# Moving the copies of bias rows and past cache behind each block's first-matrix products

## The chip, the cores and the metric

One core of one Trainium2 chip runs the whole program. The metric is device time in microseconds of one execution. The kernel before took 2709.98 us, the median of 3 runs that spread from 2709.81 to 2712.33 us.

## The reference, cut to what matters

The reference is one step of a two-layer decoder trunk on 1088 tokens (1024 of a prompt, 64 of eight running sequences) of width 1024. Layer 0 mixes with gated linear attention, layer 1 with sliding-window attention over 128 keys with a relative-position bias; both then have a squared-ReLU MLP of inner width 4096 and a gated per-layer input embedding. What the change touches is this part:

```
h = h + y                                                   # the mixer's result
h = h + square(relu(rmsnorm(h) @ w_up[i])) @ w_down[i]      # the MLP
gate = sigmoid(rmsnorm(h) @ w_ple_gate[i])
h = h + gate * (p[i] @ w_ple[i])                            # p: the per-layer input
...
bias = rel_bias.T[:, rel_bucket(max(d, 0))]                 # of layer 1's attention logits
new_k = concatenate([past_k, k_sh])[:, -n_past:]            # 120 past rows are kept, v alike
```

## The kernel before, in words

All activations are held transposed, 128 features by 1088 tokens a tile. Every product is made of three float32r products: weights and activations are split into a high and a low half, and `mm3` (L186) issues high by high (L189), high by low (L190) and low by high (L191) into the same sum. A weight tile comes by one DMA from SP into a raw buffer (2 of them), ACT casts the high half (L142), and VectorE subtracts to get the low half (L143); 5 buffers each hold the halves. `wnext` (L169) hands out the next weight tile, and fills the line so that three more tiles behind it have been asked for.

The MLP of a layer (`mlp`, L817) runs over 8 blocks of 512 inner features. A block has two parts. The first-matrix part is two calls of `up_pair` (L741). One call uses, in this order, the weight tiles A1, S2S1, C1, S4S3, A22 and C2, most of them sums of raw tiles that VectorE forms at L161 to L166; ACT and VectorE turn its results into the activations `us` (L770 to L774). The second-matrix part has eight tiles, here called down 0 to down 7, each with 36 products of 362 or 364 columns; VectorE adds each result into the residual `H` at L841, three pieces a tile. The eighth block also squares the new residual for the norm (L248, L251, L252), splits it (L221, L222) and, ahead of its second-matrix part in the program, opens the per-layer input (`ple_open`, L851): two tiles `praw` are loaded into one buffer, one after the other, each split by ACT at L218 and VectorE at L219.

In layer 0 each block also issues `bias_copies` (L929): one DMA from SP that writes two heads' bias rows 128 times (0.39 MB, memory to memory) into `ed`; the eighth block adds two copies of 120 past rows of the caches (0.98 MB each) to the outputs. GpSimd reads `ed` later in `sample_bias`, and layer 1's attention reads it.

What sets the order: `load` (L76 to L83) ties each DMA that it issues to the one before it,

```
r = self.nc.sync.dma_start(out, in_)
if self.last_load is not None:
    self.order(r.ins, self.last_load)
```

so SP issues all of them in the order of the program text. For the compute engines the framework's scheduler fixes the order of each engine's instructions when the program is built: it walks the program in its own picture of time and lets an instruction pass an earlier one that isn't ready in that picture. On the chip every engine runs its list strictly in that order.

Of the kernel before, what the change touches and what calls it, by code (L numbers as in the profile page):

```python
# [47 lines left out]
class Trunk:  # L48
# [768 lines left out]
    def mlp(self, layer, gain, utag, tags):  # L817
        nc = self.nc
        xs, rb = self.hg, self.rb
        self.hg = []  # L820
        self.pq = self.wide("pq")
        self.xz = self.rs.tile([P, TP], F32, tag="acc", name=self.uid("xz"), bufs=1)
        pt = ("mm", "gx")
        for fb in range(FB):
            us = []
            if layer == 0:
                self.bias_copies(fb)
            for f in range(0, FT, 2):
                us += [self.double(utag) for _ in range(2)]
                self.up_pair(layer, fb * FT + f, xs, us[f:])  # L830
            if fb == FB - 1:
                self.norm_begin()
                self.stx.close()
                self.ple_open(layer)
            for j in range(KT):
                ws = self.wtile([("down", layer, fb, j)])
                h = self.h[j]

                def evac(c0, cn, ps):
                    s = slice(c0, c0 + cn)  # L840
                    nc.vector.tensor_tensor(h[:, s], h[:, s], ps, op=ALU.add)  # L841
                self.gemm(ws, us, evac, kouter=(j == 0), tags=pt)
                if fb == FB - 1:
                    self.norm_add(h)
                    d = self.double(tags[j // 4])
                    self.split(d, h, self.gain(gain, j), CH if j >= 6 else ((0, T),))
                    self.hg.append(d)
        self.norm_end()
# [546 lines left out]
```

## Time and profile before

| | |
|---|---|
| median of the runs | 2709.98 us |
| profiled execution | 2710.06 us |
| its span | 2708.3 us |
| TensorE busy | 2665.8 us, 98% |
| VectorE busy | 1735.6 us, 64% |
| ScalarE (ACT) busy | 1162.2 us, 43% |
| GpSimd busy | 127.5 us, 5% |
| DMA | 163.56 MB, mean 60 GB/s |
| mean granted clock of TensorE | 0.997 of full |

The profiled execution lasts 1.8 us longer than its span, which runs from the first to the last instruction; the sum of the prediction starts from 2710.06 us. PE is TensorE's matmul, DVE is VectorE, ACT is ScalarE, POOL is GpSimd, SP the engine that issues most DMAs. A busy share says how full an engine is, not who waits: for that the list of waits, the timeline of each engine and the busy time of equal stretches are read. The layer 0 MLP lies at about 562 to 1319 us, the layer 1 MLP at about 1829 to 2571 us.

### The profile page before, as it was taken

The numbers are of one execution on the slowest core, as the hardware profiler recorded it, in microseconds if no ns is written. First come the engines' busy times: TensorE is split into PE (matmuls) and PEld (weight loads), VectorE is DVE, ScalarE is ACT, GpSimd is POOL, SyncE is SP. The second block draws the span as 40 slices with busy tenths as digits, with TensorE's granted clock in tenths as the row PEclk, the third lists the DMA queues.
The fourth block names the chain that finished last, engine by engine and source line by source line (L and its number), as shares of the span: only waits on it lengthen the run. The fifth ranks groups of instructions, "written<-read, shape, count | busy, mean of one in ns | idle before, by whom it ended". The sixth has DMA issues, their size and how long they took to land.

```text
span 2708.3 us, 46678 instructions
## 1 busy us (share of the span) xinstructions
PE 2665.8 (98%) x18369; PEld 2595.9 (96%) x18369; DVE 1735.6 (64%) x4377; ACT 1162.2 (43%) x2694; POOL 127.5 (5%) x154
## 2 busy tenths in 40 slices
PE   9999999999999999999999999999999999999997
PEld 8999999999999999999999988799999999999997
DVE  5787786584565466456755677676655655565787
ACT  5565576351232233124524666554322322332565
POOL 0000000001001000010000333200000000000000
PEclk9999999999999999999999999999999999999999
DMA  3121112311111121122122111222111111111252
GB/s 126 40 65 42 57 46 72 104 47 47 57 55 35 57 62 36 46 88 63 52 81 64 50 37 49 63 69 59 40 43 48 55 34 50 51 46 34 67 179 98
DMA packets 92801, 163.56 MB, mean 60 GB/s; under 512 B 11558, under 2 KB 30650, under 8 KB 92549
## 3 DMA queue, kind: packets, MB, share of 16 engines
q1 hardware_dynamic: 89637, 155.20, 18.6%
q10 hardware_dynamic: 1152, 4.46, 0.5%
q8 instruction: 144, 2.36, 0.4%
q0 software_dynamic: 1792, 0.92, 0.2%
q14 instruction: 76, 0.62, 0.1%
HBM read 145.95 MB, written 19.98 MB: 61 GB/s over the span
## 4 chain that ended last, share of the span: by engine, by line
PE 94%; DVE 3%; ACT 2%; issue 0%; DMA 0%; POOL 0%; DVEq 0%; SPq 0%; ACTq 0%; POOLq 0%
PE mm L191 20%; PE mm L189 20%; PE mm L190 20%; PE gx L191 8%; PE gx L190 8%; PE gx L189 8%; PE gx L549 2%; PE gx L1162 1%; PE gx L1148 1%; PE gx L578 1%; PE gx L573 1%; PE gs L1131 1%; PE gx L580 0%; PE gs L257 0%; PE gs L1132 0%
## 5 line engine op out<-in xcount | busy, mean ns | idle before, releaser
L189 PE MATMUL mm<-G,whi 128*128 128x362 f32 (+2 forms) x3160 | 1014.2, 322 | 15.7 <-ACT whi L142 9.5
L191 PE MATMUL mm<-G,wlo 128*128 128x362 f32 (+2 forms) x3160 | 1012.6, 320 | 0.8
L190 PE MATMUL mm<-G,whi 128*128 128x362 f32 (+2 forms) x3160 | 1010.8, 320 | 0.0
L189 PEld LDWEIGHTS mm<-G,whi 128*128 128x128 f32 x3160 | 594.8, 188 | 23.6 <-ACT whi L142 11.8
L191 PEld LDWEIGHTS mm<-G,wlo 128*128 128x128 f32 x3160 | 594.4, 188 | 5.4 <-DVE wlo L143 2.8
L190 PEld LDWEIGHTS mm<-G,whi 128*128 128x128 f32 x3160 | 594.9, 188 | 3.5 <-issue 1.7
L191 PE MATMUL gx<-G,wlo 128*128 128x272 f32 (+2 forms) x1304 | 397.5, 305 | 0.0
L190 PE MATMUL gx<-G,whi 128*128 128x272 f32 (+2 forms) x1304 | 397.4, 305 | 0.0
L189 PE MATMUL gx<-G,whi 128*128 128x272 f32 (+2 forms) x1304 | 397.1, 305 | 0.0
L142 ACT CAST whi<-raw 128x512 fp32r<-128x512 f32 (+1 forms) x304 | 187.2, 618 | 398.8 <-PE mm L190 318.2
L841 DVE TENSOR_TENSOR H<-H,mm 128x364 f32<-128x364 f32 (+1 forms) x256 | 135.9, 531 | 227.0 <-PE mm L191 226.3
L143 DVE TENSOR_TENSOR wlo<-raw,whi 128x512 fp32r<-128x512 f32 (+1 forms) x304 | 208.5, 687 | 73.5 <-ACT whi L142 72.7
L190 PEld LDWEIGHTS gx<-G,whi 128*128 128x128 f32 x1304 | 246.1, 189 | 0.1
L191 PEld LDWEIGHTS gx<-G,wlo 128*128 128x128 f32 x1304 | 246.1, 189 | 0.0
L189 PEld LDWEIGHTS gx<-G,whi 128*128 128x128 f32 x1304 | 245.9, 189 | 0.1
L772 ACT ACTIVATE tmp<-tmp 128x272 f32<-128x272 f32 x256 | 109.5, 432 | 270.5 <-DVE tmp L771 269.1
L841 DVE TENSOR_TENSOR H<-H,gx 128x362 f32<-128x362 f32 x128 | 68.0, 531 | 137.3 <-PE gx L191 137.2
L774 DVE TENSOR_TENSOR G<-tmp,G 128x272 fp32r<-128x272 f32 x256 | 111.5, 439 | 59.5 <-ACT G L773 58.7
L142 ACT CAST whi<-sum 128x512 fp32r<-128x512 f32 x64 | 39.5, 618 | 178.0 <-PE mm L190 150.3
L771 DVE SCALAR_TENSOR_TENSOR tmp<-tmp,rb 128x272 f32<-128x272 f32 x256 | 110.9, 437 | 3.7
L251 ACT ACTIVATE tmp<-H 128x362 f32<-128x362 f32 (+1 forms) x126 | 63.6, 507 | 114.0 <-DVE H L678 57.3
L773 ACT CAST G<-tmp 128x272 fp32r<-128x272 f32 x256 | 106.2, 419 | 5.2
(295 smaller groups left out, 4057.1 us busy)
## 6 DMA issues: line engine op xcount, KB each, us to landing
raw<-in_w_down SPq DMA_DIRECT2D x128, 256.0 KB
a<-in_w_up SPq DMA_DIRECT2D x64, 256.0 KB
raw<-in_w_up SPq DMA_DIRECT2D x64, 256.0 KB
G<-in_w_gate SPq DMA_DIRECT2D x24, 512.0 KB
raw<-in_w_o SPq DMA_DIRECT2D x32, 256.0 KB
raw<-in_w_q SPq DMA_DIRECT2D x24, 256.0 KB
x<-in_xT ACTq DMA_DIRECT2D x8, 544.0 KB
hd<-H SPq DMA_DIRECT2D x8, 544.0 KB
```

The costliest lines, as they stand in the source:

```text
L142: nc.scalar.copy(hi[:, s], raw[:, s])
L143: nc.vector.tensor_tensor(lo[:, s], raw[:, s], hi[:, s].bitcast(F32), op=ALU.subtract)
L189: mm(out, lhsT=w[0], rhs=x[0], start=first, stop=False)
L190: mm(out, lhsT=w[0], rhs=x[1], start=False, stop=False)
L191: mm(out, lhsT=w[1], rhs=x[0], start=False, stop=last)
L251: nc.scalar.activation(sq[:, :cn], h[:, s], AF.Square)
L549: nc.tensor.matmul(pp[:m, l * hw:(l + 1) * hw], lhsT=E[:, l, :m], rhs=ev[:, :, 1, :], start=True, stop=True)
L771: nc.vector.scalar_tensor_tensor(t, t, 0.0, rb[:, s], op0=ALU.max, op1=ALU.mult)
L772: nc.scalar.activation(t, t, AF.Square)
L773: nc.scalar.copy(u[:, 0, s], t)
L774: nc.vector.tensor_tensor(u[:, 1, s], t, u[:, 0, s].bitcast(F32), op=ALU.subtract)
L841: nc.vector.tensor_tensor(h[:, s], h[:, s], ps, op=ALU.add)
```

## The change

The call of `bias_copies` moves, within a block of layer 0's MLP, from ahead of the two `up_pair` calls to behind them. Nothing is added or removed.

```
         for fb in range(FB):
             us = []
-            if layer == 0:
-                self.bias_copies(fb)
             for f in range(0, FT, 2):
                 us += [self.double(utag) for _ in range(2)]
                 self.up_pair(layer, fb * FT + f, xs, us[f:])
+            if layer == 0:
+                self.bias_copies(fb)
             if fb == FB - 1:
                 self.norm_begin()
                 self.stx.close()
                 self.ple_open(layer)
```

By the order of the program, SP issues a block's copy before between the load of the first call's C1 and that of its C2, and with the change between the load of down 2 and that of down 3; in the eighth block the loads of `praw` come between the copies and down 3.

## Rows read from the trace of the kernel before

**Rows 1.** Page, the chain that ended last, by engine.

```profile
PE 94%; DVE 3%; ACT 2%; issue 0%; DMA 0%; POOL 0%; DVEq 0%; SPq 0%; ACTq 0%; POOLq 0%
```

**Rows 2.** Waits of PE, 560 to 1290: us in total, times, longest.

```profile
PE mm L189 <- ACT whi L142: 9.5, 8, 1.3
```

**Rows 3.** Stretches, one block each, layer 0 then layer 1: length, then engines' busy time.

```profile
615.00:709.79 94.79, 93.53 (x650) 93.10 (x649) 52.47 (x116) 26.62 (x60) 6.91 (x12) 1.00 0.17 50
...
1877.34:1970.33 92.99, 92.99 (x650) 92.99 (x649) 52.94 (x116) 27.09 (x60) 0.00 (x0) 1.00 0.16 46
```

**Rows 4.** Timeline of PE, layer 0: start, duration, what, idle before and its releaser.

```profile
671.48 0.29 PE L191 MATMUL gx<-tx,wlo 128*128 128x272 f32 x1
672.94 0.40 PE L189 MATMUL mm<-G,whi 128*128 128x272 f32 x1 [1.18 <-ACT whi L142]
...
673.30 0.28 PE L189 MATMUL gx<-G,whi 128*128 128x272 f32 x1
673.67 0.40 PE L191 MATMUL mm<-G,wlo 128*128 128x272 f32 x1
```

**Rows 5.** Timeline of ACT, the same moment.

```profile
671.95 0.42 ACT L773 CAST G<-tmp 128x272 fp32r<-128x272 f32 x1
672.28 0.61 ACT L142 CAST whi<-raw 128x512 fp32r<-128x512 f32 x1
```

**Rows 6.** Timeline of DVE, the same moment.

```profile
672.92 0.69 DVE L143 TENSOR_TENSOR wlo<-raw,whi 128x512 fp32r<-128x512 f32 x1
...
674.13 0.42 DVE L161 TENSOR_TENSOR sum<-a 128x256 f32<-128x256 f32 x1
```

**Rows 7.** Timeline of ACT, the same tile in layer 1.

```profile
1921.98 0.62 ACT L142 CAST whi<-raw 128x512 fp32r<-128x512 f32 x1 [2.48 <-DVE sum L165]
```

**Rows 8.** Timeline of SP, first and second block of layer 0.

```profile
523.76 0.70 SPq L78 DMA_DIRECT2D ed<-ed  x1
...
621.23 0.60 SPq L78 DMA_DIRECT2D ed<-ed  x1
626.58 0.34 SPq L78 DMA_DIRECT2D raw<-in_w_up  x1
```

**Rows 9.** Timeline of SP, layer 1: loads of down 2, 3 and 4.

```profile
1951.36 5.96 SPq L78 DMA_DIRECT2D raw<-in_w_down  x3
```

**Rows 10.** Timeline of DVE, layer 1, end of down 2.

```profile
1980.71 0.53 DVE L841 TENSOR_TENSOR H<-H,mm 128x362 f32<-128x362 f32 x1 [1.47 <-PE mm L191]
1981.19 0.69 DVE L143 TENSOR_TENSOR wlo<-raw,whi 128x512 fp32r<-128x512 f32 x1
```

**Rows 11.** Timeline of PE, layer 1: third product of down 3.

```profile
1980.85 0.33 PE L191 MATMUL mm<-G,wlo 128*128 128x364 f32 x1
```

**Rows 12.** Timeline of SP, eighth block of layer 0.

```profile
1264.94 6.11 SPq L78 DMA_DIRECT2D praw<-in_pT  x2
1271.10 0.90 SPq L78 DMA_DIRECT2D raw<-in_w_down  x2
```

**Rows 13.** Timeline of ACT, eighth block of layer 0.

```profile
1273.99 1.11 ACT L218 CAST p<-praw 128x1088 fp32r<-128x1088 f32 x1 [0.45 <-DMA praw<-in_pT]
1275.03 0.62 ACT L142 CAST whi<-raw 128x512 fp32r<-128x512 f32 x1
...
1289.98 1.19 ACT L221 ACTIVATE G<-H,gains 128x1088 fp32r<-128x1088 f32 x1
```

**Rows 14.** Timeline of DVE, eighth block of layer 0.

```profile
1269.40 1.29 DVE L219 TENSOR_TENSOR p<-praw,p 128x1088 fp32r<-128x1088 f32 x1 [0.30 <-ACT p L218]
...
1276.34 0.69 DVE L143 TENSOR_TENSOR wlo<-raw,whi 128x512 fp32r<-128x512 f32 x1
...
1291.40 1.35 DVE L222 SCALAR_TENSOR_TENSOR G<-H,gains,G 128x1088 fp32r<-128x1088 f32 x1
```

**Rows 15.** Timeline of PE, eighth block of layer 0: first product of down 3.

```profile
1288.75 0.33 PE L189 MATMUL mm<-G,whi 128*128 128x364 f32 x1
```

**Rows 16.** Stretch in layer 1's attention: length, busy times; PEclk is third from the end.

```profile
1701.76:1708.59 6.83, 6.37 (x40) 5.42 (x40) 4.62 (x20) 2.67 (x11) 1.04 (x1) 0.50 0.00 1
```

More of the change, by code (lines that the diff above doesn't have):

```diff
@@ L825, in mlp @@
             us = []
-            if layer == 0:
-                self.bias_copies(fb)
             for f in range(0, FT, 2):
@@ L830, in mlp @@
                 self.up_pair(layer, fb * FT + f, xs, us[f:])
+            if layer == 0:
+                self.bias_copies(fb)
             if fb == FB - 1:
```

## The prediction

> **What bounds the kernel now.** The chain of work that ended last comes first: TensorE holds 94% of it, so only what makes TensorE wait counts [rows 1]. The list of TensorE's waits over layer 0's MLP comes next. It has one wait of size: 8 times, 9.5 us in all, the first product of a weight tile waits for ACT's cast of that tile's high half [rows 2]. Eight blocks, eight waits. To see what they cost in all I lay a block of layer 0 beside the same block of layer 1, which has no copies, each measured from the same SP load: 94.79 against 92.99 us [rows 3]. The difference, 1.80 us a block, 14.4 us in eight, is the most that the copies' old place can give back.
>
> Then I ask why that cast is late. TensorE could have started C2 of the first call at about 671.6 us; it started at 672.94 [rows 4]. ACT ran the cast at 672.28, straight behind the cast of an activation at 671.95, which itself needed products of just before [rows 5]. In layer 1 the same cast ran at 1921.98 [rows 7]; the blocks lie 1877.34 - 615.00 = 1262.34 us apart [rows 3], so that is 659.64 on layer 0's scale, 12.6 us earlier. C2's data was not late on the chip: its load went out at 626.58 [rows 8], 45.7 us ahead of the cast. So the cast was late in ACT's written order. The scheduler put it there because in its picture C2's load, queued behind the copy, landed late. A second sign: the sums of the second call's tiles stand at 674.13 [rows 6], while in layer 1 they were done before the C2 cast, which names one of them as its releaser [rows 7]. Several loads behind the copy were late in that picture, not one.
>
> How late? The copy went out at 621.23, and C2 was due at 671.6: over 50 us. In the first block it went out at 523.76 [rows 8], C2 was due one block earlier, 671.6 - 94.8 = 576.8, and that wait is among the eight: 53 us. So the scheduler holds that what is queued behind a copy lands 53 us or more behind the copy's issue.
>
> **The change, part by part.** (1) The eight waits at C2 go, 14.4 us; the first-matrix part then looks like layer 1's. The work that covers C2 there is the cast 12 us ahead of its use.
>
> (2) The copy now stands behind down 2's load, at 1951.4 on layer 1's scale [rows 9], and ahead of down 3's. Down 3's third product, the first that needs a low half, is due at 1980.85 [rows 11]: 29 us behind the copy. In the scheduler's picture 53 us don't fit in 29. So there everything that doesn't need down 3 is placed ahead of its halves. On ACT that harms nothing in seven blocks, as ACT has no other work in the second-matrix part. On VectorE it does: the last addition of down 2 into the residual comes ahead of down 3's low half. That pair looks like the two rows at 1980.71 and 1981.19 [rows 10], and the product starts 673.67 - 672.92 = 0.75 us behind the start of its low half [rows 4, 6], so at 1981.94 instead of 1980.85: 1.09 us. One product of another piece goes first, as L189 gx does at 673.30 [rows 4], which takes 0.17 off; the restart is slow (two steps in 0.36 us from 672.94 to 673.30, where 0.25 is usual, rows 4), which adds 0.11. I take 1.03 us. The trace of before doesn't show this wait. Its bounds are 0, if the low half is placed early, and 1.80, the wait that is there now [rows 3]; 1.03 is nearer to the rows that it is built from. Seven blocks: 7.2 us. Nothing grows behind it: down 5's load waits for down 3's low half and goes out 12 us ahead of its use, more than the 3.3 us that a load took [rows 12, 13].
>
> (3) The eighth block is different. SP's list there is down 2, three copies, praw, praw again (one buffer, so behind the first one's split), down 3. In the scheduler's picture the first praw lands 53 us or more behind the copies, hence its split is placed behind all that down 0 to down 2 give: additions, squares and splits of the residual. On the chip this makes a chain in series that starts only when down 2 ends. TensorE would start down 3 at 1288.75 [rows 15]. ACT splits down 2's result at 1289.98 for 1.19 us, VectorE at 1291.40 for 1.35 [rows 13, 14]. Then the first praw's split: ACT to about 1292.2, VectorE from 1292.65 (back-to-back DVE starts overlap by some 0.1). SP's second praw issue follows that start by 1270.72 - 1269.40 = 1.32 (1270.72 is the second of two issues in a row that starts at 1264.94 and lasts 6.11, less the 0.33 of one issue): 1293.97 [rows 12, 14]. Its split on ACT follows by 1273.99 - 1270.72 = 3.27: 1297.24. Down 3's cast follows by 1.04: 1298.28 [rows 13]. TensorE starts 0.66 behind that [rows 4, 5]: 1298.94, a standstill of 10.2 us. The low half starts 1.31 behind the cast [rows 13, 14] and the product 0.75 later, at 1300.34 instead of 1289.09: 11.25 us in all. Bounds: below, the 1.03 of the other blocks; above, 11.25 and half of the second praw's 3.27 again, about 13.
>
> (4) A standstill of ten microseconds has a price in clock. The one stretch of this trace in which the clock fell inside the span's work, 6.83 us at 0.50, so 1.2 GHz, lies where TensorE had short gaps in attention [rows 16]; at half speed 6.83 us lose 3.4. Bounds 0 and 3.4; part of the dip may fall into the standstill itself, so I take 3.0. The Trainium skill, TensorE: Matmul & The Clock Gate, part 1, says that the array's default state is throttled and that activity releases it; by that the dip is certain here, and without it the sum is 3.0 less. Whether a single standstill does it no row shows.
>
> (5) What else moves: the copies' landing. GpSimd reads `ed` that much later, and nothing on the path waits for GpSimd in layer 0 [rows 2]; layer 1 reads it only in its attention, after the whole embedding stage.
>
> Sum: 2710.06 - 14.4 + 7.2 + 11.25 + 3.0 = 2717.1 us. The profiled execution is 0.08 us above the median, so no correction.
>
> **The rivals.** A, not slower: the scheduler's picture gets down 3 in time, for example because the copy's 53 us are counted from another point than its issue. Then no wait takes the place of the eight: 2710.06 - 14.4 = 2695.7. It decides at 29 us: if the copy's lateness in the picture is under that, A holds; over it, not. Against it: 53 and 50 [rows 8]. For it: the picture can't be read from the trace, only its order.
>
> B: the waits move in all eight blocks, but the eighth's chain doesn't form, because the first praw's split is placed early: 2710.06 - 14.4 + 8 x 1.03 = 2703.9. For it: praw isn't a weight and waits at 1264.94 for a buffer anyway [rows 12]. Against it: it is tied behind the copies.
>
> C: the wait at down 3 is no smaller than that at C2, because the high half is late too: 2710.06 - 14.4 + 7 x 1.80 + 11.25 + 3.0 = 2722.5. For it: TensorE waited for the high half before [rows 2]. Against it: ACT is free in the second-matrix part.
>
> D: the change doesn't do what it says; the order of the casts comes from elsewhere and stays: 2710. Against it: SP's order is tied, and layer 1, the same code without copies, has no such wait.
>
> **How the numbers follow.** Forecast 0.50, A 0.17, B 0.13, C 0.12, D 0.08. The forecast's own range is 2713 to 2721 (a wait of 0.8 to 1.3 in seven blocks, the eighth's 10 to 13, the clock's 0 to 3.4). A measurement of this kernel can tell about 0.2%, 5.4 us: faster is under 2704.6, slower over 2715.4. Faster: A and half of B, 0.24. Same: the other half of B, D and a quarter of the forecast, 0.27. Slower: the rest of the forecast and C, 0.49. The range 2702 to 2723 leaves out A and little more.
>
> **What would show it.** In the profile of the changed kernel: no wait of TensorE on the cast L142 in the first-matrix parts of layer 0, blocks there of 94.0 us; seven waits of about 1 us at down 3's L191 on VectorE's L143, right behind L841; one standstill of some 10 us in the eighth block, with ACT's L218 and SP's second praw issue behind L221 and L222; the granted clock at half behind it. Blocks of 93.0 us throughout would mean A. A first praw split ahead of down 0's L841 would mean B. A wait left at C2 would mean that the reading of the order is wrong.

## The result, and the profile after

The changed kernel took 2717.01 us, the median of 13 runs (2715.20 to 2719.34), against 2711.08 us of the kernel before (13 runs beside it, 2708.32 to 2712.61). The ratio is 1.0023, 95% interval 1.0016 to 1.0031: slower by 4 to 8 us, where 2717.1 was forecast. The profiled execution took 2716.58 us, its span 2714.8. The ratios here and below leave out one execution, of the first experiment, that took 6660.14 us.

TensorE's waits over layer 0's MLP, 560 to 1330 us, read as [rows 2] are: total, times, longest.

```profile
PE mm L189 <- ACT whi L142: 10.0, 1, 10.0
PE mm L191 <- DVE wlo L143: 6.2, 7, 0.9
```

The eight waits of 1.2 us are gone. In their place stand seven of 0.9 us, on VectorE, and one of 10 us. The stretches of [rows 3] come next; in layer 0 the length is the new step from block to block, the mean of six: the wait at L191 ends at 624.81 us in the first block and at 1189.81 in the seventh.

```profile
615.00:709.17 94.17, 93.28 (x650) 92.98 (x649) 52.98 (x116) 27.15 (x60) 6.91 (x12) 1.00 0.18 51
...
1877.34:1970.33 92.99, 92.99 (x650) 92.99 (x649) 53.08 (x117) 27.15 (x61) 0.00 (x0) 1.00 0.16 46
```

The same 650 products now take 94.17 us, not 94.79, and layer 1's stretch has not moved: a block gained 1.80 and lost 1.18. Where it lost them stands on TensorE's timeline at down 3 of the first block (the answer to [rows 11]).

```profile
623.43 0.33 PE L189 MATMUL mm<-G,whi 128*128 128x364 f32 x1
623.59 0.33 PE L190 MATMUL mm<-G,whi 128*128 128x364 f32 x1
624.81 0.43 PE L191 MATMUL mm<-G,wlo 128*128 128x364 f32 x1 [0.89 <-DVE wlo L143]
625.09 0.33 PE L189 MATMUL mm<-G,whi 128*128 128x364 f32 x1
```

Starts usually lie 0.166 us apart. The step to L191 is 1.22 and the one behind it 0.28: 1.17 us lost. VectorE's timeline shows the pair that [rows 10] stood for in layer 1, now with two weight tiles waiting behind the addition:

```profile
623.63 0.53 DVE L841 TENSOR_TENSOR H<-H,mm 128x362 f32<-128x362 f32 x1 [1.47 <-PE mm L191]
624.08 1.28 DVE L143 TENSOR_TENSOR wlo<-raw,whi 128x512 fp32r<-128x512 f32 x2
```

The data was there long before. SP issued the copy at 594.67 and down 3's load behind it; ACT cast down 3 and down 4 (the second row) 16 us ahead of the low half.

```profile
594.67 0.70 SPq L78 DMA_DIRECT2D ed<-ed  x1
596.65 32.69 SPq L78 DMA_DIRECT2D raw<-in_w_down  x5
```
```profile
607.66 1.14 ACT L142 CAST whi<-raw 128x512 fp32r<-128x512 f32 x2
```

VectorE had idled 1.47 us just ahead of that addition with the low half's inputs ready. It is the written order that made it wait, as at C2 before. C2's cast itself stands again where layer 1 has it: at 659.09, where [rows 7] less one layer gave 659.64.

In the eighth block the chain formed. SP, then ACT, then VectorE, answering [rows 12, 13, 14]:

```profile
1254.47 2.21 SPq L78 DMA_DIRECT2D out_kcs<-in_kpast  x1
1256.73 0.69 SPq L78 DMA_DIRECT2D out_vcs<-in_vpast  x1
1258.77 29.16 SPq L78 DMA_DIRECT2D praw<-in_pT  x2
1287.98 11.45 SPq L78 DMA_DIRECT2D raw<-in_w_down  x5
```
```profile
1283.81 1.19 ACT L221 ACTIVATE G<-H,gains 128x1088 fp32r<-128x1088 f32 x1
1284.90 1.08 ACT L218 CAST p<-praw 128x1088 fp32r<-128x1088 f32 x1
1291.10 1.10 ACT L218 CAST p<-praw 128x1088 fp32r<-128x1088 f32 x1 [5.12 <-DMA praw<-in_pT]
1292.10 1.13 ACT L142 CAST whi<-raw 128x512 fp32r<-128x512 f32 x2
```
```profile
1285.02 1.35 DVE L222 SCALAR_TENSOR_TENSOR G<-H,gains,G 128x1088 fp32r<-128x1088 f32 x1 [0.56 <-ACT G L221]
1286.29 1.28 DVE L219 TENSOR_TENSOR p<-praw,p 128x1088 fp32r<-128x1088 f32 x1
1292.23 1.29 DVE L219 TENSOR_TENSOR p<-praw,p 128x1088 fp32r<-128x1088 f32 x1 [4.65 <-ACT p L218]
1293.44 1.29 DVE L143 TENSOR_TENSOR wlo<-raw,whi 128x512 fp32r<-128x512 f32 x2
```

SP's two praw issues are one group of 29.16 us: the first at 1258.77, the second at 1258.77 + 29.16 - 0.33 = 1287.60, because it waits for the first one's split, which the written order holds back until down 2's squares and splits are done. TensorE:

```profile
1282.41 0.32 PE L191 MATMUL mm<-G,wlo 128*128 128x362 f32 x1
1292.77 0.67 PE L189 MATMUL mm<-G,whi 128*128 128x364 f32 x1 [10.04 <-ACT whi L142]
...
1294.18 0.67 PE L191 MATMUL mm<-G,wlo 128*128 128x364 f32 x1
```

Last, two stretches of this block; PEclk is third from the end.

```profile
1286.45:1296.69 10.24, 3.92 (x12) 3.62 (x13) 3.62 (x4) 2.14 (x3) 0.00 (x0) 0.50 0.45 150
1292.77:1296.74 3.97, 3.97 (x12) 3.67 (x13) 1.95 (x3) 0.47 (x1) 0.00 (x0) 0.51 0.41 120
```

TensorE's granted clock stood at 0.50, which is 1.2 GHz, for 10.24 us, but 6.3 of these lie in the standstill, where there was nothing to slow down. The twelve products in what is left took 3.97 us where twelve steps of 0.166 take 2.0. In layer 1's attention this execution has a drop like that of [rows 16], 6.83 us at 0.50 from 1716.53, so that drop doesn't enter the difference.

### The profile page after: what moved, and what is told of

It reads as the page before. It is cut to its first block, busy times and chain, and to the rows that moved or that the text cites. A ratio compares the mean times of both kernels' runs of the same rounds, so it can differ in the third digit from the quotient of the medians.

```text
span 2714.8 us, 46703 instructions
## 1 busy us (share of the span) xinstructions
PE 2665.9 (98%) x18369; PEld 2595.9 (96%) x18369; DVE 1738.3 (64%) x4377; ACT 1166.4 (43%) x2694; POOL 127.6 (5%) x154
## 4 chain that ended last, share of the span: by engine, by line
PE 95%; DVE 2%; ACT 1%; issue 1%; DMA 0%; POOL 0%; DVEq 0%; SPq 0%; ACTq 0%; POOLq 0%
PE mm L191 20%; PE mm L189 20%; PE mm L190 20%; PE gx L190 8%; PE gx L189 8%; PE gx L191 8%; PE gx L549 2%; PE gx L1148 1%; PE gx L1162 1%; PE gx L578 1%; PE gx L573 1%; PE gs L1131 1%; PE gs L257 0%; PE gx L580 0%; PE gs L1132 0%
## 5 line engine op out<-in xcount | busy, mean ns | idle before, releaser
L189 PE MATMUL mm<-G,whi 128*128 128x362 f32 (+2 forms) x3160 | 1015.7, 322 | 16.6 <-ACT whi L142 10.0
L191 PE MATMUL mm<-G,wlo 128*128 128x362 f32 (+2 forms) x3160 | 1014.4, 321 | 6.4 <-DVE wlo L143 6.2
L189 PEld LDWEIGHTS mm<-G,whi 128*128 128x128 f32 x3160 | 596.4, 189 | 23.1 <-ACT whi L142 10.9
L191 PEld LDWEIGHTS mm<-G,wlo 128*128 128x128 f32 x3160 | 595.7, 189 | 11.6 <-DVE wlo L143 9.1
L191 PE MATMUL gx<-G,wlo 128*128 128x272 f32 (+2 forms) x1304 | 397.9, 305 | 0.0
L189 PE MATMUL gx<-G,whi 128*128 128x272 f32 (+2 forms) x1304 | 397.9, 305 | 0.0
L142 ACT CAST whi<-raw 128x512 fp32r<-128x512 f32 (+1 forms) x304 | 186.4, 618 | 481.2 <-PE mm L190 220.8
L841 DVE TENSOR_TENSOR H<-H,mm 128x364 f32<-128x364 f32 (+1 forms) x256 | 136.0, 531 | 243.5 <-PE mm L191 242.8
L143 DVE TENSOR_TENSOR wlo<-raw,whi 128x512 fp32r<-128x512 f32 (+1 forms) x304 | 207.1, 687 | 90.9 <-ACT whi L142 90.8
L189 PEld LDWEIGHTS gx<-G,whi 128*128 128x128 f32 x1304 | 246.4, 189 | 0.1
L191 PEld LDWEIGHTS gx<-G,wlo 128*128 128x128 f32 x1304 | 246.5, 189 | 0.0
L841 DVE TENSOR_TENSOR H<-H,gx 128x362 f32<-128x362 f32 x128 | 67.8, 530 | 120.2 <-PE gx L191 120.2
L142 ACT CAST whi<-sum 128x512 fp32r<-128x512 f32 x64 | 39.5, 617 | 158.6 <-PE mm L190 131.2
```

The lines of the kernel that those rows point to most:

```text
L142: nc.scalar.copy(hi[:, s], raw[:, s])
L143: nc.vector.tensor_tensor(lo[:, s], raw[:, s], hi[:, s].bitcast(F32), op=ALU.subtract)
L189: mm(out, lhsT=w[0], rhs=x[0], start=first, stop=False)
L191: mm(out, lhsT=w[1], rhs=x[0], start=False, stop=last)
```

## The experiments

The theory: the price is set by where the scheduler writes casts and low halves, and it does so because it takes a load queued behind such a copy to be late; its own times can't be seen. The first rival: the loads are really late, because the copies hold the DMA queue. The second, for the eighth block: the two cache copies' 2 MB cost by themselves. Unless another kernel is named, a diff is against the changed kernel. The kernel before ran beside each; its median was 2710.84 us beside the kernels that move only one part of the copies, reshape the bias copy alone, or use GpSimd; 2711.84 beside the reshaped copies at the old place and the last experiment; 2711.16 beside the others.

**Copies of the eighth block behind the first praw's load.** Is it the two praw loads behind the copies that make the chain?

```
-            if layer == 0:
+            if layer == 0 and fb < FB - 1:
                 self.bias_copies(fb)
             if fb == FB - 1:
                 ...
                 self.ple_open(layer)
+                if layer == 0:
+                    self.bias_copies(fb)
```

> The changed kernel, but in the eighth block the copies are issued behind the two loads of the per-layer input instead of ahead of them. Theory (the order written at build time, in which whatever is queued behind a copy is taken to be late): the series of split, second load, split and cast goes, with its standstill of 10.2 us and the half-clock stretch behind it; 12.3 us go, a wait like that of the other blocks or somewhat longer comes back (1.2 to 4 us): 2717.0 - 12.3 + 1.2 to 4 = 2706 to 2709 us, a ratio to the kernel before of 0.998 to 0.999. The seven waits of 1.18 us stay. Rival (the three copies really keep the DMA rings busy, so down 3's data is late on the chip): the copies still stand ahead of down 3's load, so a standstill of near 10 us stays, 2715 to 2718 us.

2711.86 us, ratio to the kernel before 1.0001 (0.9992 to 1.0011). The 10 us chain is gone, the seven waits stay (6.2 in all), but in the eighth block one of 4.2 us is left, and 3.41 us at half clock behind it. TensorE's waits, SP, and ACT:

```profile
PE mm L191 <- DVE wlo L143: 6.2, 7, 0.9
PE mm L189 <- ACT whi L142: 4.2, 1, 4.2
```
```profile
1267.80 0.68 SPq L78 DMA_DIRECT2D out_vcs<-in_vpast  x1
1268.52 23.59 SPq L78 DMA_DIRECT2D raw<-in_w_down  x5
```
```profile
1285.43 1.38 ACT L142 CAST whi<-raw 128x512 fp32r<-128x512 f32 x2 [1.26 <-DMA raw<-in_w_down]
```

This cast does wait for its data, 17 us after down 3's load went out directly behind the cache copies. So here the rival is partly right: 1.26 us of ACT's wait is a transfer. The median lies 3 us over the upper end of the expectation, and the eighth block accounts for it: down 3's first product started at 1286.10, 4.34 us late (down 2's last had started at 1281.59), and it and those behind it ran mostly at half clock. Length and TensorE's busy time up to the first product back at full clock:

```profile
1286.10:1289.93 3.83, 3.83 (x12) 3.40 (x13) 1.37 (x2) 0.62 (x1) 0.78 (x2) 0.55 0.53 143
```

Twelve products took 3.83 us instead of 2.0. The block loses 6.2 us, where 1.2 to 4 were expected, and 2711.16 - 14.4 + 8.3 + 6.2 = 2711.3 is the median within 0.6. The profiled execution (2708.02) is faster than that by about the drop of the clock in layer 1's attention, estimated at 3.4 us in the one of before [rows 16]: it had none, and the same place reads 1.00. The runs of this kernel divide the same way: up to 2709.71 us at a mean granted clock of 0.996 or 0.997, from 2710.68 us at 0.994 or 0.995.

```profile
1690.00:1710.00 20.00, 17.00 (x150) 12.06 (x149) 16.36 (x70) 13.30 (x50) 4.92 (x5) 1.00 0.18 48
```

**The order alone.** Same transfers, same places; a constraint puts down 3's low half ahead of down 2's last addition in seven blocks. At L143 and at L841:

```
-                    nc.vector.tensor_tensor(lo[:, s], raw[:, s], hi[:, s].bitcast(F32), op=ALU.subtract)
+                    r = nc.vector.tensor_tensor(lo[:, s], raw[:, s], hi[:, s].bitcast(F32), op=ALU.subtract)
+                    self.los[k] = r.ins
...
-                    nc.vector.tensor_tensor(h[:, s], h[:, s], ps, op=ALU.add)
+                    r = nc.vector.tensor_tensor(h[:, s], h[:, s], ps, op=ALU.add)
+                    if layer == 0 and fb < FB - 1 and j == 2 and c0 == CH[2][0]:
+                        self.order(r.ins, self.los[("down", layer, fb, 3)])
```

> The changed kernel with the same transfers in the same places, but in seven blocks an order edge alone puts the low half of down 3 ahead of the last addition of down 2 on VectorE. Theory: the seven waits at down 3 come from VectorE's order, not from data; they vanish, 7 x 1.18 = 8.3 us: 2717.0 - 8.3 = 2708.7 us, and the eighth block's standstill stays. Rival (data late behind a real transfer): the waits stay, 2717 us.

2707.63 us, ratio 0.9984 (0.9975 to 0.9993). TensorE's waits (two added lines move L142 to L143 and L189 to L191):

```profile
PE mm L191 <- ACT whi L143: 9.8, 1, 9.8
```

VectorE now runs down 3's low half at 623.42 and the addition behind it, at 624.97. All seven waits are gone with the same transfers in the same places: they came from VectorE's order, not from the data. Against the changed kernel that is 0.0039 of 2711, 10.6 us, some 2 more than 7 x 1.18; the intervals together allow that.

**A second bias copy in seven blocks.** Doubles the bytes and the queue's load.

```
         self.load(self.ed[s], self.ed1[s].unsqueeze(1).broadcast_to([2, P, 384]))
+        if i < FB - 1:
+            self.load(self.ed2[s], self.ed1[s].unsqueeze(1).broadcast_to([2, P, 384]))
```

> The changed kernel with a second copy of the same size, into scratch memory, behind the first in seven blocks: the suspected transfer doubled (nothing reads the second). Theory: the order is already as late as it can be made, and the chip has slack, as down 3 was cast at 607.7 and due at 623.4: the waits stay at 1.2 us, 2717 us within 2. Rival (real transfer time sets the wait): each wait grows by about one copy's 8 to 10 us, 7 x 9 = 63 us, 2780 us; a half-way case, with contention alone, 2719 to 2725.

2715.46 us, ratio 1.0019 (1.0010 to 1.0028); the waits are 6.2 in seven and 9.8 in one. Twice the copy costs nothing that could be told: the low half already stood behind the addition, and the waits, which end with an instruction of VectorE, did not grow with the transfer.

**Only the first seven blocks moved, and only the eighth.** In the first kernel the eighth block's call stays at its old place, in the second the other seven do.

```
+            if layer == 0 and fb == FB - 1:          # the second kernel: fb < FB - 1
+                self.bias_copies(fb)
             for f in range(0, FT, 2):
                 ...
-            if layer == 0:
+            if layer == 0 and fb < FB - 1:           # the second kernel: fb == FB - 1
                 self.bias_copies(fb)
```

> One part of the change alone: the copies of the first seven blocks move, the eighth block's stay ahead of its first-matrix part. Theory: seven waits of 1.80 become seven of 1.18, the eighth keeps its 1.80 at C2: 2711.1 - 7 x 0.62 = 2706.8 us, ratio 0.9984; no standstill, no half-clock stretch in the layer 0 MLP. Rival (the change's cost lies in all blocks alike): 2711.1 + 7/8 of 6 = 2716 us.

2706.68 us, ratio 0.9986 (0.9977 to 0.9995).

> The other part alone: only the eighth block's copies move. Theory: seven waits of 1.80 stay at C2, the eighth's goes and the standstill with its half-clock stretch comes, 12.3 us: 2711.1 - 1.8 + 12.3 = 2721.6 us, ratio 1.0039. Rival (cost alike in all blocks): 2711.1 + 6/8 = 2712 us.

2722.49 us, ratio 1.0044 (1.0031 to 1.0058). The waits of the one and of the other:

```profile
PE mm L191 <- DVE wlo L143: 6.2, 7, 0.9
PE mm L189 <- ACT whi L142: 1.2, 1, 1.2
```
```profile
PE mm L189 <- ACT whi L142: 18.2, 8, 9.9
```

Each part carries its own price: -0.0014 and +0.0044 make +0.0030 where both together measured 0.0023 (0.0016 to 0.0031). Seven blocks of the change are a gain of 4 us, the eighth loses about 12. In the second kernel seven waits of 1.2 stand beside one of 9.9.

**The copies' shape.** The bias copy has two heads outermost, the cache copies eight sequences. This writes the long dimension outermost, the same bytes from and to the same places: first in all three at the new place, then in the bias copy alone at the old place, then in all three at the old place.

```
-        self.load(self.ed[s], self.ed1[s].unsqueeze(1).broadcast_to([2, P, 384]))
+        self.load(self.ed[s].rearrange("h p c -> p h c"),
+                  self.ed1[s].unsqueeze(1).broadcast_to([2, P, 384]).rearrange("h p c -> p h c"))
...
-                self.load(self.O[out][:, 0:120, :], self.I[past][:, 8:128, :])
+                self.load(self.O[out][:, 0:120, :].rearrange("b k e -> k b e"),
+                          self.I[past][:, 8:128, :].rearrange("b k e -> k b e"))
```

> The changed kernel with the same bytes copied, but all three kinds of copy written with their long dimension (128 or 120 rows) outermost instead of 2 or 8. Theory: the copy's length in the build-time picture comes from how few pieces its outermost dimension gives; with 128 pieces it ends within the 29 us that down 3 has, so no engine's order changes against layer 1, all waits go: 2717.0 - 8.3 - 12.3 = 2696.4 us, ratio to the kernel before 0.9946. Blocks of layer 0 take 93.0 us. Rival (any memory-to-memory copy ahead of a load makes it late, whatever its shape): 2717 us.

2697.11 us, ratio 0.9949 (0.9937 to 0.9961); over layer 0's MLP one wait of 0.2 us is left, none of it for weights. The cache copies' 2 MB stand ahead of down 3's load here as in the changed kernel, so the second rival, that these bytes cost by themselves, falls; what their transfer costs in the old shape, the last experiment asks.

> The kernel before, copies in their old place, but the bias copy alone is written with its 128 rows outermost; the two cache copies keep 8 pieces. Theory: the place is not the cause, the shape is: the seven waits at C2 vanish, the eighth, behind the cache copies, keeps its 1.80: 2711.1 - 12.6 = 2698.5 us, ratio 0.9954. Rival (the place ahead of the block is what costs): 2711 us.

2696.99 us, ratio 0.9951 (0.9937 to 0.9964); of [rows 2] only the eighth block's wait is left:

```profile
PE mm L189 <- ACT whi L142: 1.2, 1, 1.2
```

> The copies at their old place, all three written with their long dimension outermost; nothing else. Theory (the scheduler's lateness comes from the shape of a copy, not its bytes): the last wait, 1.2 us at C2 of the eighth block, goes as well, no wait of TensorE is left in layer 0's MLP, and the time is that of the run with only the bias copy spread, 2697.0, less 1.2 to 1.8 us: about 2695.5. Rival (the two cache copies are late for their bytes, 0.98 MB each): the 1.2 us wait at C2 of the eighth block stays, 2697.0.

2694.07 us, ratio 0.9937 (0.9923 to 0.9950); that wait is gone too, and TensorE is busy through the stretch in which the changed kernel had 93.28 us of work:

```profile
615.00:709.17 94.17, 94.17 (x657) 94.17 (x656) 53.51 (x117) 27.08 (x60) 6.92 (x12) 1.00 0.18 53
```

This beats both kernels, the one before by 0.6%. With this shape the place no longer matters that could be told: 0.9949 and 0.9937, each within 0.0014. The shape also changes the transfer. GB/s in 40 slices of 0.275 us, each view from just before the copy's issue in the block of [rows 3], in the kernel before (621 to 632 us, issue at 621.23) and with the three reshaped copies at the old place (619 to 630, issue at 619.12):

```profile
GB/s 0 0 15 141 156 290 305 67 56 45 56 45 56 45 56 45 56 45 56 45 56 45 56 74 130 45 108 276 384 164 56 45 56 45 56 45 60 45 15 0
```
```profile
GB/s 0 0 0 89 179 380 354 298 302 324 291 106 50 11 0 0 0 0 0 0 0 31 82 60 52 328 397 76 31 30 5 0 5 0 46 15 4 1 5 0
```

The peaks of the first view are the weight loads ahead of the copy and behind it. Between them the copy with two pieces outermost crawls at 45 to 56 GB/s, while the same view's busy share of the 16 DMA engines reads 1 tenth. With 128 outermost the copy and the load ahead of it, 0.65 MB together, are through at some 300 GB/s, with that share mostly at 8 or 9 tenths. The Trainium skill, DMA: Bandwidth & Descriptors, section Rules for kernel authors, says that an outermost dimension smaller than 16, a leading broadcast among its examples, confines a DMA to at most that many engines. The two rates and shares agree with it. Yet in the kernel before even the slow copy was through by 632 us, 40 us ahead of the cast that stood too late. What cost TensorE its 1.8 us was the place that the cast was given in the order, not the copy's time on the chip; the run with the order alone says the same for the new place.

**The copies issued by GpSimd, their call at the old place and in the old shape.** Takes them out of SP's queue.

```
-        self.load(self.ed[s], self.ed1[s].unsqueeze(1).broadcast_to([2, P, 384]))
+        self.nc.gpsimd.dma_start(self.ed[s], self.ed1[s].unsqueeze(1).broadcast_to([2, P, 384]))
...
-                self.load(self.O[out][:, 0:120, :], self.I[past][:, 8:128, :])
+                self.nc.gpsimd.dma_start(self.O[out][:, 0:120, :], self.I[past][:, 8:128, :])
```

> The kernel before, copies in their old place and shape, issued from GpSimd instead of SP, so that no weight load is queued behind one on SP. Theory: the lateness comes from standing in one queue with the loads; all eight waits go: 2711.1 - 14.4 = 2696.7 us, ratio 0.9947. Rival (the transfers themselves, on the same rings' engines, cost): 2711 us, or between where they slow loads on the chip.

2702.00 us, ratio 0.9967 (0.9954 to 0.9979): no wait is left in layer 0's MLP, but 5 us are missing. Outside `load` nothing ties these DMAs, and the scheduler moved all ten of them ahead of the MLP: the cache copies to 2.55 and 40.41 us, the eight bias copies to 446.58 up to 529.54. GpSimd (two of each kind), and TensorE's second product, which the kernel before starts at 6.85:

```profile
2.55 0.60 POOL L937 DMA_DIRECT2D out_kcs<-in_kpast  x1
40.41 0.57 POOL L937 DMA_DIRECT2D out_vcs<-in_vpast  x1
446.58 1.10 POOL L934 DMA_DIRECT2D ed<-ed  x1 [1.93 <-DMA ed<-rows]
529.54 1.07 POOL L934 DMA_DIRECT2D ed<-ed  x1 [11.25 <-issue]
```
```profile
11.33 0.67 PE L189 MATMUL mm<-G,whi 128*128 128x362 f32 x1 [5.64 <-ACT G L221]
```

So the waits go when no copy stands among the weight loads, but this run doesn't tell a copy's place in SP's queue from its transfer, since no copy runs beside the MLP here; the runs above do that. 4.5 of the 5 us lie at the start. That the cache copy slows the first input loads there is likely from the times, but no run kept all else and moved it away.

**What is left in the eighth block.** The first experiment again, with the cache copies alone reshaped.

```
             (against the first experiment's kernel)
-                self.load(self.O[out][:, 0:120, :], self.I[past][:, 8:128, :])
+                self.load(self.O[out][:, 0:120, :].rearrange("b k e -> k b e"),
+                          self.I[past][:, 8:128, :].rearrange("b k e -> k b e"))
```

> As the run with the eighth block's copies behind the per-layer input's first load, with the two cache copies alone written with their long dimension outermost; the bias copies keep their shape. Theory 1 (the 4.2 us standstill in the eighth block comes from the transfers: down 3's load runs beside 2 MB of cache copies): the standstill stays at 3 to 5 us with a dip of the clock, the time stays at 2709 to 2712. Theory 2 (it comes from the written order or from the shape of the cache copies): it falls to the 0.9 us of the other blocks, the clock stays at full, and the time falls by some 5 us, to about 2706.

2710.58 us, ratio 0.9996 (0.9987 to 1.0005). Neither expectation is met in full. TensorE's waits, and ACT:

```profile
PE mm L191 <- DVE wlo L143: 6.8, 8, 0.9
PE mm L189 <- ACT whi L142: 2.8, 1, 2.8
```
```profile
1283.97 1.19 ACT L221 ACTIVATE G<-H,gains 128x1088 fp32r<-128x1088 f32 x1
1285.06 1.12 ACT L142 CAST whi<-raw 128x512 fp32r<-128x512 f32 x2
1290.35 0.62 ACT L142 CAST whi<-raw 128x512 fp32r<-128x512 f32 x1 [4.17 <-DMA raw<-in_w_down]
```

Down 3's cast no longer waits for data, it stands straight behind the residual's split: what is left of the wait, 2.8 us, is written order (the bias copy ahead of it kept its old shape). So of the 4.2 us some 1.3 were the transfer of the cache copies and the rest order. The time did not fall with it, within 0.1%, because half clock lasted 6.82 us here instead of 3.41. The stretch from down 3's first product to the first one back at full clock:

```profile
1285.72:1292.75 7.03, 6.44 (x20) 5.96 (x21) 3.16 (x5) 1.49 (x3) 0.00 (x0) 0.51 0.26 77
```

The first product came 2.98 us late (down 2's last had started at 1282.57), and twenty products took 7.03 us instead of 3.3: 6.7 us lost in this block, against 6.2 in the first experiment. Why the shorter standstill had the longer stretch at half clock no run shows.

## Why the prediction was right

The direction, the place of every wait and the mechanism of each were right. Two sizes were off in opposite directions, the seven waits by +1.1 us and the chain with its clock by -2.0; that the sum came so close, 2717.1 against 2717.01, is in part luck.

- Step 1, the eight waits at C2: -14.4 forecast. The list of waits has none there, and a block less the 1.17 us lost on TensorE's timeline is 94.17 - 1.17 = 93.00 us, where layer 1's takes 92.99.
- Step 2, a wait in seven blocks: 1.03 each was forecast, 1.18 measured (94.17 - 92.99), 8.3 us instead of 7.2. The low half began 624.81 - 624.08 = 0.73 us ahead of its product, as taken. The 0.17 that I took off for a product of another piece going first was wrong: TensorE's order has none ahead of this L191.
- Step 3, the chain: the standstill came out at 10.36 - 0.17 = 10.19 us, 10.2 forecast, link by link: second praw issue 1.31 behind VectorE's split (1.32 forecast), its split on ACT 3.50 later (3.27), down 3's cast 1.00 later (1.04), the product 0.67 later (0.66). L191 was due at 1282.41 + 3 x 0.166 = 1282.91 and started at 1294.18, 11.27 late (11.25); but here two products did go ahead of it, which gives 0.33 back.
- Step 4, the clock: 3.0 forecast. The whole eighth block lost 10.19 + (3.97 - 2.0) = 12.2 us, so the clock's part beside the chain's 10.94 (11.27 - 0.33) is about 1.2. The half clock set in during the standstill and more than half of it was over before TensorE had work. The bound of 3.4 came from a dip that fell on work [rows 16]; for a long wait that is not the nearest row. The rule cited there, of the Trainium skill's TensorE: Matmul & The Clock Gate, part 1, held in the sense taken: the dip came with this single standstill.
- Sum by the measured terms: 2710.06 - 14.4 + 8.3 + 12.2 = 2716.2; the profiled execution took 2716.58.

Rival A fell on the seven waits, B on the chain, C on the wait's 1.18 us, D on the empty first-matrix part. Of the reason given, that the scheduler takes what is queued behind a copy to land 53 us or more behind it, the runs show the sense (what needs a load behind a copy of this shape is written late, in either place, and is not with the copy in another shape or gone from among the loads) and not the figure, since its times aren't in any trace.

## What to carry to other kernels

Where an engine waits for an instruction that had its data long before, the wait sits in the written order, and moving the DMA that caused it can move the wait to the next tile behind it, as it did here; that cost more in the one block where the next tile led a chain of load, split and load. Mend the cause first: writing the copies with their long dimension outermost gave 0.6%, where the best change of place alone gave 0.14%.
A change that acts in a loop has to be priced in its last round by itself: seven blocks gained 4 us and the eighth lost 12.

## What the runs showed that was not expected

- The length of a half-clock stretch is not the length of the standstill that it comes with: 3.41 us with 4.2, 6.82 with 2.8, 10.24 with 10.0, and none with the seven waits of 0.9. What it costs depends on how much of it falls on work: the products behind the standstill lost 1.8 us with the stretch of 3.41 and 3.7 with that of 6.82 (a 0.6 us wait for the low half included), but 2.0 with that of 10.24.
- The drop in layer 1's attention comes and goes between executions and kernels: 6.83 us in the one of before [rows 16], none in that of the first experiment. At 3.4 us it is as large as the differences between the smaller experiments, so those are read from the medians, not from a single profiled execution.
